# HGRN2 scores of all seven levels in one group of column-tiled products, from kept copies of keys and queries

## The chip, the cores and the metric

One Trainium2 chip, one of its cores, one launch. The metric is the device time of an execution in microseconds (us), as the median of several runs. Beside it stands one profiled execution, whose trace gives the start and the length of every instruction on every engine: PE (TensorE matmul), PEld (TensorE weight load), DVE (VectorE), ACT (ScalarE), POOL (GpSimd) and SP, the queue that issues nearly all DMAs.

## What is computed

One layer of a decoder trunk for 272 prompt positions (16 learned meta tokens and 256 prompt tokens) and 8 sampled tokens, of width 2048: a feed-forward half, a mixer, a second feed-forward half, each followed by a layer norm. All matrices are float32. The mixer projects its input to ten parts of width 2048 and runs two branches on them, retention and HGRN2, whose gated sum goes through an output projection. The change lies in HGRN2, which has 16 heads of width 128. Cut to what matters, a head computes over the prompt:

```python
b = cumsum(log f)                                   # f: forget gate, one value per position and channel
A[i, j] = sum_d q[i, d] * k[j, d] * exp(b[i, d] - b[j, d])      for j <= i, else 0
o = A @ v + (q * exp(b)) @ S                        # S: the state from earlier positions
```

The scores A are what the change touches. The decay between positions i and j differs by channel, so A isn't one product of q and k.

## The kernel before, in words

**The dense work.** Every weight matrix is streamed once, in units of eight 128x128 blocks (512 KB). SP loads a unit into `raw` (L185), ACT casts it to the reduced format `whi` (L188), DVE subtracts to get the remainder `wlo` (L189), and PE multiplies each block three times (L218: whi by xh, whi by xl, wlo by xh). Each of raw, whi and wlo has three buffers, so a unit can't be loaded, cast or subtracted before PE is done with the unit three earlier. Results go to PSUM and are evacuated by ACT and DVE.

**The mixer.** `project` (L629) walks through the parts of the input projection for eight pairs of heads, u = 0 to 7: for each pair the groups f, q_h, i_h, q_r, k_r, v_r, and then the gates of the pair before. A group is 16 steps k of `dense`; after each step `pump` (L617) is called. In the rest of the text a pump is such a step, six dense matmuls. The work of a pair that isn't dense is written as two Python generators, `mix_hg` (HGRN2) and `mix_ret` (retention). A `yield n` puts the rest of the generator off by n pumps. So the yields set, by hand, where in PE's order each small product stands; PE executes strictly in that order. The instructions of DVE, ACT, POOL and SP are put in order ahead of time by a scheduler: each engine's list follows the order of writing, but an instruction whose inputs are ready early, by the scheduler's own reckoning, may be placed earlier. On the chip each engine then works through its list in order.

**The scores.** They are built over seven levels s = 1, 2, 4, ... 64. At level s the positions fall into blocks of 2s; the queries of the second half of a block meet the keys of its first half. K and Q hold keys and queries scaled so far. After the products of a level, `scale_k(s)` and `scale_q(s)` (DVE, recorded at L240) multiply K and Q in place by the gates of that level, and `join(s)` forms the gates of the next. Because the scaling is in place, a level's products have to be done before it.

- `side_by_side(s)` (L799) copies what three levels need of Q into a tile Qm (Q1 for levels 1, 2; Q4 for 4, 8), side by side, so that one product gives three of them.
- `blocks(Q1, 1, q)` (L811, called at L859) issues, per head and half, column-tiled products: 32 columns of keys as weights, at column j of the array (tile_position (0, j)). Its second moving operand, q, gives the pairs within a block. DVE then spreads the results into the score tile acc with one product with the identity (L828) and three predicated copies (L834) for each head. `blocks(Q4, 4)` (L866) does the same for levels 4 and 8.
- Levels 16, 32 and 64 (L874 to L904) have each a PSUM bank of their own: products of 16, 32 or 64 key columns (L886, L881), the scaling, and ACT copies into acc (L899, L894). After levels 16 and 32, `load` (L765) issues two 512 KB DMAs for one of the two heads: vbh (a broadcast of sampled values) and smh (the state of the sampled sequences).

Each fp32 product is two records in the trace. The five places stand at these pumps after the generator's start, for every u: Q1 at 14, Q4 at 27, level 16 at 39, level 32 at 47, level 64 at 55. The transposes of K (L917) follow at 63, with the update of smh on ACT (L927) and DVE (L928). The tag smh has two buffers, shared by Q1, Q4 and the two smh; the tag vbh has two, for the two vbh.

**Retention beside it.** `mix_ret` is a second generator, started after v_r. It loads two smr tiles of 512 KB each for a first and again for a second half of the sampled states (L1010), vbr tiles of 256 KB (L1070), updates smr on ACT (L1106) and DVE (L1112) and writes them out (L1116). For u = 0 and u = 1 its start and that of mix_hg are set differently from the later ones (L670, L686), so that in these two pairs the two generators overlap more.

Of the kernel before, what the change touches and what calls it, by code (L numbers as in the profile page):

```python
# [14 lines left out]
ALU = mybir.AluOpType  # L15
# [3 lines left out]
P = 128  # L19
# [109 lines left out]
def trunk(ctx: ExitStack, tc: tile.TileContext, A, O):  # L129
# [417 lines left out]
    with tc.tile_pool(name="yp", bufs=1) as yp:  # L547
# [7 lines left out]
        with tc.tile_pool(name="mp", bufs=1) as mp:  # L555
# [190 lines left out]
            def mix_hg(u, f, k, q, v):  # L746
# [52 lines left out]
                def side_by_side(s):  # L799

                    x = tmp("Qm", (P, 3, 2 * P), tag="smh", bufs=2)
# [9 lines left out]
                def blocks(x, s, own=None):  # L811

                    x = x.rearrange("p i (x j c) -> p i x j c", x=4, j=4)
                    for h in range(2):
                        pl = mx_bank("pl")
                        half = pl[:, : 2 * 80].rearrange("p (b c) -> p b c", b=2)
                        for b in range(2):
                            for mine in range(1 if own is None else 2):
                                for j in range(0, P, 32):
                                    at = b * P + j  # L820
                                    o, y = half[j : j + 32, b, :48].rearrange("p (i c) -> p i c", i=3), x[:, :, 2 * h + b, j // 32, :]
                                    if mine:
                                        o, y = half[j : j + 32, b, 48:], own[:, h, at : at + 32]
                                    nc.tensor.matmul(
                                        o, K[:, h, NMETA + at : NMETA + at + 32], y, start=True, stop=True, tile_position=(0, j))
                        a = acc[:, 2 * P * h : 2 * P * (h + 1)]
                        if own is not None:
                            nc.vector.tensor_tensor(  # L828
                                out=a.rearrange("p (b j c) -> p b j c", b=2, j=4),
                                in0=half[:, :, 48:].unsqueeze(2).to_broadcast([P, 2, 4, 32]),  # L830
                                in1=ident.rearrange("p (j c) -> p j c", j=4).unsqueeze(1).to_broadcast([P, 2, 4, 32]), op=ALU.mult)
                        for i, (sl, mi) in enumerate(((s, MASKS[s][0]), (2 * s, MASKS[2 * s][0]), (2 * s, MASKS[2 * s][1]))):
                            n = 16 // sl
                            nc.vector.copy_predicated(  # L834
# [39 lines left out]
                for s in LEVELS[MASKED:]:  # L874
# [27 lines left out]
                    if s in (16, 32):  # L902
                        load(s // 32)
# [387 lines left out]
```

## Time and profile before

| | |
|---|---|
| median of 3 runs | 2581.47 us (2581.25 to 2583.45) |
| the profiled execution's own time | 2582.39 us |
| its span, first to last instruction | 2580.6 us |
| PE, PEld busy | 99%, 98% of the span |
| DVE, ACT, POOL busy | 66%, 53%, 2% |
| DMA | 536.25 MB, 208 GB/s over the span |

The span starts with the first instruction of the program; all times of the trace count from there. Matmuls are pipelined: a dense matmul's record is 0.28 us long but the next one starts about 0.12 us later, so the records overlap and the busy share of PE says little. What a piece of work costs PE is read from the distance between starts. The mixer with the input projection lies between about 780 and 1770 us.

### The profile page before, as it was taken

Reading aid. Unit: us, or ns where it says so; the run is one execution under the profiler, and the core shown is the slowest. Engines: PE = TensorE matmul, PEld = TensorE weight load, DVE = VectorE, ACT = ScalarE, POOL = GpSimd, SP = SyncE. Lnnn points to the kernel's source line nnn. Section 1 sums busy time; section 2 is a strip of 40 time slices with the busy share of each in tenths; the row PEclk is TensorE's granted clock in tenths of the full one; section 3 lists DMA queues with packets and bytes.
Section 4 is the critical chain, followed back from the end, with each engine's and each line's share of the span. In section 5 each row is a group of like instructions: output and inputs, shape, how many; then the busy total and the mean of one; then the engine's idle time right before and its main releaser. Section 6 shows DMA issues by size and latency. Waiting matters only on the chain.

```text
span 2580.6 us, 55997 instructions
## 1 busy us (share of the span) xinstructions
PE 2565.8 (99%) x23360; PEld 2540.0 (98%) x23360; DVE 1702.4 (66%) x2827; ACT 1378.0 (53%) x2146; POOL 46.4 (2%) x112
## 2 busy tenths in 40 slices
PE   9999999999999999999999999999999999999999
PEld 9999999999999999999999999999999999999998
DVE  6454454475579887777777878787985555556555
ACT  5444444444456665757575757575564444444444
POOL 0000000000000000000000000000000000000000
PEclk9999999999999999999999999999999999999999
DMA  7555555555566786767676767676666666666664
GB/s 242 182 186 184 184 187 181 188 181 184 184 200 216 248 276 208 262 211 257 213 255 216 253 220 254 215 236 195 196 186 199 196 197 195 195 194 194 196 196 149
DMA packets 156895, 536.25 MB, mean 208 GB/s; under 512 B 17952, under 2 KB 25952, under 8 KB 156640
## 3 DMA queue, kind: packets, MB, share of 16 engines
q1 hardware_dynamic: 156352, 532.37, 64.0%
q8 instruction: 183, 3.00, 0.5%
q14 instruction: 72, 0.59, 0.1%
q10 hardware_dynamic: 288, 0.29, 0.0%
HBM read 501.99 MB, written 30.61 MB: 206 GB/s over the span
## 4 chain that ended last, share of the span: by engine, by line
PE 93%; DVE 3%; DMA 2%; ACT 1%; issue 1%; SPq 0%; DVEq 0%; ACTq 0%
PE up L218 34%; PE dn L218 19%; PE pj_v_r L218 4%; PE pj_i_h L218 3%; PE pj_g_r L218 3%; PE wo L218 3%; PE pj_q_r L218 3%; PE pj_f L218 3%; PE pj_k_r L218 3%; PE pj_a_r L218 3%; PE pj_g_h L218 3%; PE pj_a_h L218 3%; PE pj_q_h L218 3%; DVE wlo L189 1%; DMA raw<-in_w_up 1%
## 5 line engine op out<-in xcount | busy, mean ns | idle before, releaser
L189 DVE TENSOR_TENSOR wlo<-raw,whi 128x1024 fp32r<-128x1024 f32 (+1 forms) x869 | 1061.8, 1222 | 762.5 <-ACT whi L188 760.8
L188 ACT CAST whi<-raw 128x1024 fp32r<-128x1024 f32 (+1 forms) x870 | 906.0, 1042 | 935.3 <-PE up L218 408.3
L218 PE MATMUL up<-xh,wlo 128*128 128x280 f32 (+1 forms) x2624 | 725.9, 280 | 1.0 <-DVE wlo L189 1.0
L218 PE MATMUL up<-xh,whi 128*128 128x280 f32 (+1 forms) x2624 | 725.7, 280 | 0.5 <-ACT whi L188 0.4
L218 PE MATMUL up<-xl,whi 128*128 128x280 f32 (+1 forms) x2624 | 725.4, 279 | 0.0
L218 PEld LDWEIGHTS up<-xh,wlo 128*128 128x128 f32 x2624 | 492.6, 189 | 1.9 <-DVE wlo L189 1.9
L218 PEld LDWEIGHTS up<-xh,whi 128*128 128x128 f32 x2624 | 492.6, 189 | 0.9 <-ACT whi L188 0.9
L218 PEld LDWEIGHTS up<-xl,whi 128*128 128x128 f32 x2624 | 492.6, 189 | 0.0
L218 PE MATMUL dn<-hh,whi 128*128 128x280 f32 (+1 forms) x1376 | 384.7, 280 | 0.0
L218 PE MATMUL dn<-hh,wlo 128*128 128x280 f32 (+1 forms) x1376 | 384.3, 279 | 0.0
L218 PE MATMUL dn<-hl,whi 128*128 128x280 f32 (+1 forms) x1376 | 384.3, 279 | 0.0
L218 PEld LDWEIGHTS dn<-hh,whi 128*128 128x128 f32 x1376 | 260.1, 189 | 0.1
L218 PEld LDWEIGHTS dn<-hl,whi 128*128 128x128 f32 x1376 | 260.1, 189 | 0.1
L218 PEld LDWEIGHTS dn<-hh,wlo 128*128 128x128 f32 x1376 | 260.1, 189 | 0.0
L218 PE MATMUL pj_g_r<-xh,whi 128*128 128x264 f32 x256 | 76.5, 299 | 0.0
L218 PE MATMUL pj_g_h<-xh,whi 128*128 128x264 f32 x256 | 74.2, 290 | 0.0
L218 PE MATMUL pj_k_r<-xh,whi 128*128 128x280 f32 x256 | 73.8, 288 | 0.0
L218 PE MATMUL pj_v_r<-xh,whi 128*128 128x280 f32 x256 | 73.4, 287 | 0.0
L218 PE MATMUL pj_v_r<-xh,wlo 128*128 128x280 f32 x256 | 72.4, 283 | 0.3 <-DVE wlo L189 0.3
L218 PE MATMUL pj_k_r<-xh,wlo 128*128 128x280 f32 x256 | 72.4, 283 | 0.0
L218 PE MATMUL pj_k_r<-xl,whi 128*128 128x280 f32 x256 | 72.3, 283 | 0.0
L218 PE MATMUL pj_v_r<-xl,whi 128*128 128x280 f32 x256 | 72.3, 283 | 0.0
(408 smaller groups left out, 5242.4 us busy)
## 6 DMA issues: line engine op xcount, KB each, us to landing
raw<-in_w_up SPq DMA_DIRECT2D x343, 512.0 KB
raw<-in_w_in SPq DMA_DIRECT2D x320, 512.0 KB
raw<-in_w_dn SPq DMA_DIRECT2D x172, 512.0 KB
smr<-in_sr SPq DMA_DIRECT2D x32, 512.0 KB
out_srs<-smr SPq DMA_DIRECT2D x32, 512.0 KB
raw<-in_w_out SPq DMA_DIRECT2D x32, 512.0 KB
smh<-in_sg SPq DMA_DIRECT2D x16, 512.0 KB
vbr<-vrd SPq DMA_DIRECT2D x32, 256.0 KB
```

The costliest lines, as they stand in the source:

```text
L188: nc.scalar.copy(hi[:, j:jn, :], raw[:, j:jn, :])
L189: nc.vector.tensor_tensor(out=lo[:, j0:j1, :], in0=raw[:, j0:j1, :], in1=hi[:, j0:j1, :].bitcast(F32), op=ALU.subtract)
L218: nc.tensor.matmul(o, w, t, start=start, stop=stop)
```

## The change

The products of all seven levels are moved to one place, pump 40 (45 for u = 0, where those of Q1 stay at pump 14). So that the scaling can go on before that, the operands of each level are kept:

- for u > 0, the products with Q1 and q take the unscaled keys k in place of K;
- a tile `kept`, in one of the two vbh buffers, holds a copy of K for levels 4 and 8 (K4) and the keys of levels 16 and 32; the queries of levels 16 and 32 go to a fourth part of Q1 and Q4 (the tile fills its buffer as smh does). These are five ACT copies for each u: one of 512 columns and four of 256;
- level 64 uses K and Q as they then are.

`upper` issues levels 16, 32 and 64, with at most 32 key columns in a product: the 64 columns of level 64 are split in two. All results share two PSUM banks. `fill` (the DVE part of the old blocks) and `keep` (the ACT copies of levels 16 to 64) come after, spread over 8 pumps; both `load` calls come right behind the products; the yields again add up to 63 pumps before the transposes of K.

```diff
-                    x = tmp("Qm", (P, 3, 2 * P), tag="smh", bufs=2)
+                    x = tmp("Qm", (P, 4, 2 * P), tag="smh", bufs=2)
...
-                def blocks(x, s, own=None):
-
-                    x = x.rearrange("p i (x j c) -> p i x j c", x=4, j=4)
+                def blocks(half, x, keys, h, own=None):
+
+                    x = x[:, :3].rearrange("p i (x j c) -> p i x j c", x=4, j=4)
...
+                                if mine:
+                                    o, y = half[j : j + 32, b, 48:], own[:, h, at : at + 32]
+                                nc.tensor.matmul(o, keys[:, h, at : at + 32], y, start=True, stop=True, tile_position=(0, j))
+
+                def fill(half, s, h):
+                    a = acc[:, 2 * P * h : 2 * P * (h + 1)]
+                    if s == 1:
+                        nc.vector.tensor_tensor(
...
+                    for i, (sl, mi) in enumerate(((s, MASKS[s][0]), (2 * s, MASKS[2 * s][0]), (2 * s, MASKS[2 * s][1]))):
...
+                def upper(pl, s, keys, qs):
+
                     for h in range(2):
                         for b in range(2):
+                            o = (h if s == 64 else 2 * h + b) * s
+                            for j in range(0, P, 2 * s):
+                                y = qs(h, b, j)
+                                for i in range(0, s, 32):
+                                    r = 64 * b + i if s == 64 else j
+                                    w = min(s, 32)
                                     nc.tensor.matmul(
-                                        o, K[:, h, NMETA + at : NMETA + at + 32], y, start=True, stop=True, tile_position=(0, j))
-                        a = acc[:, 2 * P * h : 2 * P * (h + 1)]
...
+                                        pl[r : r + w, o : o + s], keys(h, b, j)[:, i : i + w], y,
+                                        start=True, stop=True, tile_position=(0, r))
+
+                def keep(pl, s):
+                    if s == 64:
+                        for b in range(2):
+                            nc.scalar.copy(
...
-                blocks(Q1, 1, q)
+                kept = tmp("kept", (P, 4, 2 * P), tag="vbh", bufs=2)
+                K4 = kept[:, :2, :]
+                pls = [None, None]
+                first = lambda h: pls[h][:, : 2 * 80].rearrange("p (b c) -> p b c", b=2)
+                second = lambda h: pls[h][:, 2 * 80 : 2 * 128].rearrange("p (b c) -> p b c", b=2)
+                if u == 0:
+                    for h in range(2):
+                        pls[h] = mx_bank("pl")
+                        blocks(first(h), Q1, K[:, :, NMETA:], h, q)
+                        fill(first(h), 1, h)
                 scale_q(2)
                 join(2)
                 Q4 = side_by_side(4)
                 scale_k(1)
                 scale_k(2)
-                yield 2 * W_LEVEL - 1 + calm
-                blocks(Q4, 4)
+                yield W_LEVEL + calm
+                nc.scalar.copy(K4, K[:, :, NMETA:])
                 join(4)
...
-                yield W_LEVEL + 4 + calm
-                for s in LEVELS[MASKED:]:
-                    pl = mx_bank("pl")
-                    for h in range(2):
-                        for b in range(2):
-                            k0, q0, o = NMETA + b * P, b * P, (2 * h + b) * s
-                            if s == 64:
-                                j = 64 * b
...
-                                    pl[j : j + s, h * s : (h + 1) * s], K[:, h, k0 : k0 + s], Q[:, h, q0 + s : q0 + 2 * s],
...
-                                    nc.tensor.matmul(
-                                        pl[j : j + s, o : o + s], K[:, h, k0 + j : k0 + j + s],
-                                        Q[:, h, q0 + j + s : q0 + j + 2 * s], start=True, stop=True, tile_position=(0, j))
+                yield W_LEVEL
+                held = {}
+                for i, s in enumerate((16, 32)):
+                    held[s] = kept[:, 2 + i, :], (Q1, Q4)[i][:, 3, :]
+                    nc.scalar.copy(
+                        held[s][0].rearrange("p (h n s) -> p h n s", h=2, s=s),
+                        K[:, :, NMETA:].rearrange("p h (n t s) -> p h n t s", t=2, s=s)[:, :, :, 0, :])
+                    nc.scalar.copy(held[s][1].rearrange("p (h n s) -> p h n s", h=2, s=s), odd(s))
                     scale_k(s)
                     scale_q(s)
                     join(s)
-                    if s == 64:
-                        for b in range(2):
-                            nc.scalar.copy(
...
-                            nc.scalar.copy(
-                                acc[j * s : (j + 1) * s, :].rearrange("p (x n s) -> p x n s", x=4, s=s)[:, :, j + 1, :],
-                                pl[j * s : (j + 1) * s, : 4 * s].rearrange("p (x s) -> p x s", x=4))
-                    if s in (16, 32):
-                        load(s // 32)
-                    yield W_LEVEL + calm
+                    yield W_LEVEL if i == 0 or u else W_LEVEL + 5
+                for h in range(2):
+                    if u or pls[0] is None:
+                        pls[h] = mx_bank("pl")
+                        blocks(first(h), Q1, k[:, :, NMETA:], h, q)
+                if u == 0:
+                    pls = [mx_bank("pl") for h in range(2)]
+                for h in range(2):
+                    blocks(second(h), Q4, K4, h)
+                tops = {16: pls[0][:, 256:320], 32: pls[0][:, 320:448], 64: pls[1][:, 256:384]}
+                for s in (16, 32):
+                    at = lambda h, b, j: slice(128 * h + (b * P + j) // 2, 128 * h + (b * P + j) // 2 + s)
+                    upper(tops[s], s, lambda h, b, j: held[s][0][:, at(h, b, j)], lambda h, b, j: held[s][1][:, at(h, b, j)])
+                upper(
+                    tops[64], 64, lambda h, b, j: K[:, h, NMETA + b * P : NMETA + b * P + 64],
+                    lambda h, b, j: Q[:, h, b * P + 64 : (b + 1) * P])
+                scale_k(64)
+                scale_q(64)
+                join(64)
+                for h in range(2):
+                    load(h)
+                for h in range(2):
+                    if u:
+                        fill(first(h), 1, h)
+                    fill(second(h), 4, h)
+                    yield 4
+                for s in (16, 32, 64):
+                    keep(tops[s], s)
+                yield 15 if u else 10
```

47 lines of the change are left out of this document (20 added, 27 removed).

## The prediction

> **What bounds the kernel now.** I read the page first, its span and its chain of work:
>
> ```profile
> span 2580.6 us, 55997 instructions
> PE 93%; DVE 3%; DMA 2%; ACT 1%; issue 1%; SPq 0%; DVEq 0%; ACTq 0%
> ```
>
> The chain that ended last is PE for 93%. Then I read the busy time by stage, for a pair of heads in the middle of the mixer (u = 3), and PE's own waits:
>
> ```profile
> 1095.00:1223.00 128.00, 128.00 (x1271) 125.53 (x1270) 98.42 (x194) 82.14 (x152) 5.55 (x9) 1.00 0.72 236
> ...
> PE pl L881 <- DVE Q L240: 3.3, 1, 3.3
> ```
>
> The columns of the first row are length, then busy time of PE, PEld, DVE, ACT and POOL, the granted clock, DMA share and GB/s. PE has no hole in 128 us. Its longest wait of the whole span, in the second row, is one of 3.3 us in the pair u = 1. So what is taken out of PE's list for u = 2 to 7 comes off the end, as long as nothing else becomes late; for u = 0 and 1 that has to be seen.
>
> What the five places cost PE is read from the timeline of PE, u = 3: the last dense matmul before, the products, the dense matmuls after.
>
> ```profile
> 1140.96 0.28 PE L218 MATMUL pj_k_r<-xh,wlo 128*128 128x280 f32 x1
> 1141.17 0.29 PE L824 MATMUL pl<-Qm,K 128*32 128x48 f32 x8
> ...
> 1141.72 0.27 PE L824 MATMUL pl<-q,K 128*32 128x32 f32 x8
> 1141.92 0.39 PE L218 MATMUL pj_k_r<-xh,whi 128*128 128x280 f32 x1
> 1142.14 0.28 PE L218 MATMUL pj_k_r<-xl,whi 128*128 128x280 f32 x1
> ...
> 1151.08 0.28 PE L218 MATMUL pj_k_r<-xl,whi 128*128 128x280 f32 x1
> 1151.20 0.28 PE L218 MATMUL pj_k_r<-xh,wlo 128*128 128x280 f32 x1
> 1151.41 0.55 PE L824 MATMUL pl<-Qm,K 128*32 128x48 f32 x32
> 1151.89 0.39 PE L218 MATMUL pj_k_r<-xh,whi 128*128 128x280 f32 x1
> 1152.11 0.28 PE L218 MATMUL pj_k_r<-xl,whi 128*128 128x280 f32 x1
> ...
> 1160.45 0.28 PE L218 MATMUL pj_v_r<-xh,wlo 128*128 128x280 f32 x1
> 1160.67 0.39 PE L886 MATMUL pl<-Q,K 128*16 128x16 f32 x32
> 1161.20 0.28 PE L218 MATMUL pj_v_r<-xl,whi 128*128 128x280 f32 x1
> ...
> 1166.61 0.28 PE L218 MATMUL pj_a_r<-xh,wlo 128*128 128x264 f32 x1
> 1166.82 0.45 PE L886 MATMUL pl<-Q,K 128*32 128x32 f32 x16
> 1167.41 0.28 PE L218 MATMUL pj_g_r<-xl,whi 128*128 128x264 f32 x1
> ...
> 1174.93 0.28 PE L218 MATMUL pj_a_r<-xh,wlo 128*128 128x264 f32 x1
> 1175.14 0.45 PE L881 MATMUL pl<-Q,K 128*64 128x64 f32 x8
> 1175.73 0.28 PE L218 MATMUL pj_g_r<-xl,whi 128*128 128x264 f32 x1
> ```
>
> Dense matmuls start 0.12 us apart (1151.08, 1151.20), some 0.11 among the gates, which have 264 columns and not 280. From the last dense start before a group to the second one after it lie two such steps and the group's cost. Q1: 1142.14 - 1140.96 - 0.24 = 0.94. Q4: 0.91 - 0.24 = 0.67. Level 16: 0.75 - 0.24 = 0.51. Level 32: 0.80 - 0.22 = 0.58. Level 64 the same, 0.58. Together 3.28 us for each pair of heads.
>
> **The change, part by part.** *Joining the groups.* For Q4, the first product starts 0.21 after the dense one ahead of it, not 0.12, and the dense matmul behind has 0.22 to the next, not 0.12: 0.19 for going in and out. The length of one record gives the tail:
>
> ```profile
> L824 PE MATMUL pl<-Qm,K x512: 206/206/230, 817.7 to 1662.8; 128*32 128x48 f32 x171
> L834 DVE COPY_PREDICATED acch<-msk,pl x96: 283/364/508, 819.1 to 1664.2; 128x128 f32<-128x128 uint8 x96
> ```
>
> The last of the 32 records started at 1151.41 + 0.55 - 0.21 = 1151.75, so the next dense one came 0.14 behind it, while four records side by side take 0.34 / 8 = 0.04. Some 0.10 of that tail goes when another level follows at once. So a join saves 0.29, and for u = 1 to 7 there are four: 1.16. Level 64 changes from 8 records to 16. By Q4's pace (0.34 / 32) 16 records take 0.18, by their own of today (0.23 for 8) 0.46, against 0.23; I take no difference, nearest to Q4, since these too are 32-column tiles. I take **1.15 us saved per pair, between 0.9 and 1.2**; for u = 0, three joins, 0.9.
>
> *The copies.* Each pair adds five ACT copies; the nearest rows, by tile, and the stage in which they can lie, u = 5 ahead of the group:
>
> ```profile
> L755 ACT COPY K<-k x8: 627/646/659, 781.3 to 1622.9; 128x544 f32<-128x544 f32 x8
> L803 ACT COPY Qm<-Q x16: 399/418/455, 804.7 to 1635.5; 128x256 f32<-128x256 f32 x16
> ...
> 1518.00:1545.00 27.00, 27.00 (x342) 26.45 (x341) 20.60 (x43) 10.37 (x14) 2.39 (x2) 1.00 0.77 253
> 1545.00:1550.00 5.00, 5.00 (x45) 5.00 (x43) 1.79 (x3) 2.78 (x6) 0.00 (x0) 1.00 0.45 131
> 1550.00:1555.00 5.00, 5.00 (x59) 4.83 (x57) 3.77 (x6) 3.91 (x11) 0.99 (x1) 1.00 0.56 197
> ```
>
> One copy of 0.65 and four of 0.42 are 2.3 us of ACT, which is busy for 10.4 of 27 there: cost nothing, hidden by dense matmuls. Without that cover a pair pays up to 2.3. The scaling no longer waits for products when u > 0, so the chain can run early; behind a waiting ACT copy stand the whi casts.
>
> *The DVE work that moves.* The fills (12 predicated copies of 0.36 and two products with the identity of about the same for each pair, some 5.1 us by records) go from pumps 14 and 27 to pumps 40 to 48. The rows 1545 to 1555 show DVE busy for 5.56 of 10 us: 4.4 free. Four scalings of levels 16 and 32 leave that stretch, at some 0.4 each. So 5.1 comes, 1.6 goes, 4.4 is free, less the 1.15 PE gains: it fits by nothing. What is late next is the row pair
>
> ```profile
> 1574.85 1.22 DVE L189 TENSOR_TENSOR wlo<-raw,whi 128x1024 fp32r<-128x1024 f32 x1
> 1576.18 0.33 PE L218 MATMUL pj_g_r<-xh,wlo 128*128 128x264 f32 x1
> ```
>
> of the timeline: wlo ends at 1576.07, and PE uses it 0.11 later. The scalings of level 64 (0.8) also move ahead of this busy stretch, which helps. I take no stall; the bound is all that PE saves, 1.15 per pair.
>
> *The loads.* `kept` holds one vbh buffer and the fourth parts of Q1 and Q4 hold smh till the group is done, so three of the four 512 KB loads can't start sooner. Now, by SP's timeline (u = 5):
>
> ```profile
> 1518.19 1.09 SPq L769 DMA_DIRECT2D vbh<-vh0d  x1
> ...
> 1525.33 0.33 SPq L770 DMA_DIRECT2D smh<-in_sg  x1
> ```
>
> They start some 20 us sooner than they will. For u = 2 to 7 the rows above show DMA busy 0.45 and 0.56 of the time behind the group, and the loads have 23 pumps (16 us): nothing. In SP's list raw loads stand behind those waiting loads; three buffers cover them. For u = 0 and 1 it is tighter:
>
> ```profile
> 835.67 6.27 DMA smr<-in_sr
> 845.31 1.24 DVE wlo L189
> ...
> 940.94 4.14 DMA vbr<-vrd
> 948.40 0.45 PE pl L881 x8
> ...
> 831.00:847.00 16.00, 14.78 (x180) 13.91 (x179) 12.24 (x28) 12.75 (x22) 1.81 (x4) 1.00 0.92 305
> 935.00:940.00 5.00, 5.00 (x58) 4.83 (x57) 4.91 (x11) 4.94 (x9) 0.82 (x2) 1.00 0.97 355
> ```
>
> Here the chain leaves PE: for u = 0 through smr, which holds up ACT and with it whi and wlo (PE is busy 14.78 of 16, 1.2 idle); for u = 1 through vbr, which held up DVE and thereby the scaling that level 64 waited for (the 3.3). Moved out from before these waits, the loads free the smr of u = 0; moved to about 933 and 847 (estimates, where levels 16 and 32 of these two pairs stand now), 1.5 MB at 355 GB/s are 4.4 us of a DMA that is 0.92 to 0.97 busy. Level 64's own wait goes with u = 1; the same late DMA may hold up wlo instead. I count 0.6 of the 2.05 that PE saves in these two pairs, with bounds of -6.6 (all saved and both waits gone) and +4.
>
> **Sum:** 6 x 1.15 + 0.6 = 7.5. The profiled execution took 2582.4 itself, 1.8 more than its span, and so becomes 2574.9; it stood 0.9 above the median, so the median becomes **2574.0**.
>
> **The rivals.**
>
> *The waits of u = 0 and 1 go too.* For it: level 64 no longer stands behind vbr, and smr lands earlier. Against: both waits come from DMAs, which don't get fewer. 6.9 + 6.6 = 13.5, limited by what wlo allows to about 12: 2569.
>
> *The gain is eaten by DVE or by the moved loads.* The 0.11 speaks for it, and 4.4 us of DMA in each of two crowded pairs; against it the free DVE time before and the slack of later pairs. If DVE takes half in each pair and the loads the rest: about 2579; if all, 2581.5.
>
> *One long group runs at a slower pace than short ones (slower).* In place, the point is (3.28 - 0.3) / 160 = 18.6 ns per record, 160 being the records of the joined group. Q1, the longest run so far, does 64 records in 1141.72 + 0.27 - 0.2 - 1141.17 = 0.62, or 10 ns each, and speaks against it. Level 32, at 16 in 0.37 to the next dense one, shows 23 ns. If issue fell to that after the first 64, or all along, a group would take 4.0 and each pair 0.7 more: 2587.
>
> The Trainium skill, "TensorE: Matmul & The Clock Gate", section "Wait — 56ns, not 53.3ns?", says that matmuls never start closer than about 25 ns, however small. By that figure, as an estimate, 160 records take 4.0 and the time would be about 2589. This case's trace disagrees: Q1's 64 start 10 ns apart, in four column tiles.
>
> **How the numbers follow.** A measurement here can tell about 0.2% from no change, 5.2 us: faster is below 2576.3, slower above 2586.6. Forecast (2571 to 2577): 0.45, nearly all faster. Waits gone (2567 to 2571): 0.17. Eaten (2577 to 2583): 0.29. Slow pace: 0.07; other mishaps, slower: 0.02. So faster 0.62, same 0.29, slower 0.09. From 2568 to 2582 some 0.8 are held.
>
> **What would show it.** In the profile after, a group of 160 records that takes PE 2.0 to 2.3 us, once per pair; the distance of equal places of u = 3 and u = 4 down by 1.1 to 1.2; PE still without holes from 1095 on; ACT copies hidden. It is wrong if the group has gaps or a wait in its middle, if the list of PE's waits shows wlo or whi in each pair, or if waits on smr, vbr or smh in the first two pairs exceed the 4.5 us of now.

## The result, and the profile after

The changed kernel takes 2603.58 us (median of 5 runs, 2601.14 to 2606.48), the kernel before beside it 2582.12 (5 runs, 2581.25 to 2583.45): a ratio of 1.0083, with an interval of 1.0069 to 1.0096. The forecast was 2574.0, in a range of 2568 to 2582. The change makes the kernel 21.5 us slower where 8 us less was expected. The profiled execution took 2606.48 us.

The span and the chain of the page, after:

```profile
span 2604.7 us, 56181 instructions
PE 82%; DVE 7%; ACT 6%; DMA 3%; issue 2%; POOL 0%; SPq 0%; DVEq 0%; ACTq 0%
```

PE's share of the chain falls from 93% to 82%: operands now come late. PE's waits name them (total, times, longest):

```profile
PE pt L1063 <- ACT v L684: 12.0, 6, 2.6
PE pj_g_h L218 <- DVE wlo L189: 7.1, 8, 1.4
PE pt L1070 <- ACT acch L859: 1.9, 5, 0.4
PE pj_g_r L218 <- DVE wlo L189: 1.6, 2, 1.2
...
PE pt L874 <- POOL ends L751: 0.9, 2, 0.7
```

The longest is new and comes six times, once for each pair from u = 2 on: the first transpose of retention (L1063) waits for ACT to copy v_r out of PSUM (L684). A wait for wlo at L218 comes in each of these pairs too.

**The group itself** does what was forecast. PE's timeline, u = 5:

```profile
1428.18 0.28 PE L218 MATMUL pj_v_r<-xh,wlo 128*128 128x280 f32 x1
1428.39 0.29 PE L821 MATMUL pl<-Qm,k 128*32 128x48 f32 x8
...
1429.87 0.41 PE L847 MATMUL pl<-Q,K 128*32 128x64 f32 x14
1430.21 0.39 PE L218 MATMUL pj_v_r<-xh,whi 128*128 128x280 f32 x1
1430.43 0.28 PE L218 MATMUL pj_v_r<-xl,whi 128*128 128x280 f32 x1
```

From the last dense start before it to the second after it are 2.25 us; less two steps of 0.12, the group costs 2.01, against 3.28 for the five places. So 1.27 us a pair is saved. Its 160 records start within 1428.39 and 1429.87 + 0.41 - 0.24 = 1430.04: 1.65 us, 10 ns each. The Trainium skill, "TensorE: Matmul & The Clock Gate", section "Wait — 56ns, not 53.3ns?", has a floor of about 25 ns between starts; this trace disagrees for tiles of 16 and 32 columns, over 160 records as over 64.

**Where the time went** is seen from equal places of two pairs. The products of level 16, u = 4 and u = 5, before (name, times, shortest/median/longest, first and last start):

```profile
L886 PE MATMUL pl<-Q,K x32: 176/176/189, 1288.7 to 1288.9; 128*16 128x16 f32 x32
...
L886 PE MATMUL pl<-Q,K x32: 176/176/189, 1416.4 to 1416.6; 128*16 128x16 f32 x32
```

and the start of the group after for u = 4; that for u = 5 stands above, at 1428.39:

```profile
L821 PE MATMUL pl<-Qm,k x32: 206/208/231, 1296.9 to 1297.5; 128*32 128x48 f32 x32
```

A pair took 127.7 us before and takes 131.5 after. With the 1.27 saved, about 5 us of this pair are waits. (The rows of before from 1518 to 1576, which the prediction calls u = 5, are of u = 6, by the count of Q1's places in the trace; nothing in it hangs on the number.)

**What ACT does behind the group.** Its timeline before, u = 5 (start, length, and in brackets the idle time ahead and what ended it):

```profile
1420.97 0.39 ACT L684 COPY v<-pj_v_r 128x280 f32<-128x280 f32 x1 [1.63 <-PE pj_v_r L218]
1421.26 1.05 ACT L188 CAST whi<-raw 128x1024 fp32r<-128x1024 f32 x1
1422.21 0.40 ACT L685 COPY v<-pj_v_r 128x280 f32<-128x280 f32 x1
...
1434.22 0.99 ACT L927 ACTIVATE smh<-smh,fs 128x128 f32<-128x128 f32 x3
```

and after:

```profile
1431.11 1.05 ACT L188 CAST whi<-raw 128x1024 fp32r<-128x1024 f32 x1 [3.83 <-PE pj_v_r L218]
1435.40 1.28 ACT L968 ACTIVATE smh<-smh,fs 128x128 f32<-128x128 f32 x4 [3.24 <-DMA smh<-in_sg]
1436.58 1.03 ACT L188 CAST whi<-raw 128x1024 fp32r<-128x1024 f32 x1
1437.63 0.39 ACT L684 COPY v<-pj_v_r 128x280 f32<-128x280 f32 x1
1437.92 0.40 ACT L685 COPY v<-pj_v_r 128x280 f32<-128x280 f32 x1
```

Before, the updates of smh came 13 us behind the copies of v_r. Now the first four stand ahead of them, and ACT stands idle 3.24 us for the DMA that fills smh.

Two things lie behind that. The first is what lets the updates go: they are scaled by the tile `fs`, which by its tag is put into the buffer of T64, the gates of level 64. So POOL can write fs only when the scaling of level 64 has read them. That scaling now follows the group at once:

```profile
1430.76 0.42 DVE L240 TENSOR_TENSOR Q<-Q,T 128x256 f32<-128x256 f32 x1
```

POOL starts fs at 1431.24, right behind it, 6.4 us ahead of the copy of v_r; before, it started 13.0 us behind that copy. The second is the load. SP issued it only after the group, since Q1 and Q4 held its buffers (before, the two loads of smh went out at 1397.67 and 1408.38):

```profile
1429.86 0.33 SPq L770 DMA_DIRECT2D smh<-in_sg  x1
...
1430.72 0.43 SPq L770 DMA_DIRECT2D smh<-in_sg  x1
```

Issued at 1429.86, used at 1435.40: 5.5 us. Behind the waiting update stand a cast of whi, and with it a wlo, and the copies of v_r. PE's timeline shows the bill:

```profile
1435.80 0.28 PE L218 MATMUL pj_a_r<-xh,wlo 128*128 128x264 f32 x1
1438.08 0.44 PE L1063 MATMUL pt<-ident,v 128*128 128x128 f32 x2 [2.00 <-ACT v L684]
...
1442.16 0.44 PE L1070 MATMUL pt<-ident,k_r 128*128 128x128 f32 x2 [0.39 <-ACT acch L859]
...
1461.87 0.38 PE L218 MATMUL pj_g_h<-xh,wlo 128*128 128x264 f32 x1 [1.00 <-DVE wlo L189]
```

Measured by how far the same dense matmul stands behind its place in the trace of before, the steps of this pair are +2.2 at the v transposes, +0.6 at the second k transposes (a PSUM bank is free only after the score copies), +0.4 at the sums with ks, +1.2 at wlo and, ahead of the group, +0.4 at the transpose of `ends`: 4.8, less 1.27.

The same measure for every run below, from the two traces (the dense matmuls are the same in all of them). It counts from the first matmul of f of u = 0 to the output projection, cut in the group q_r of u = 2:

| run | median, us | ratio to before, with interval | u = 0 and 1, us against before | each of u = 2 to 7 |
|---|---|---|---|---|
| the changed kernel | 2603.58 | 1.0083 (1.0069 to 1.0096) | +1.0 | +3.88 |
| late_scale64 | 2587.57 | 1.0022 (1.0012 to 1.0031) | +0.3 | +0.88 |
| keep_first | 2601.58 | 1.0071 (1.0056 to 1.0086) | +1.2 | +2.94 |
| no_fill | 2602.05 | 1.0070 (1.0055 to 1.0085) | +2.5 | +2.82 |
| before_late_loads | 2582.04 | 1.0000 (0.9991 to 1.0009) | -0.2 | +0.04 |
| level64_apart | 2589.91 | 1.0035 (1.0023 to 1.0046) | +7.4 | -0.22 |
| level64_apart_no_fill | 2587.25 | 1.0021 (1.0011 to 1.0030) | +10.5 | -0.43 |
| two_groups | 2599.79 | 1.0071 (1.0054 to 1.0088) | +11.6 | +0.98 |
| before_early_updates | 2591.50 | 1.0050 (1.0028 to 1.0072) | +5.4 | +0.65 |
| gated | 2595.07 | 1.0044 (1.0031 to 1.0058) | +5.6 | +1.25 |
| gated_no_fill | 2587.66 | 1.0020 (1.0011 to 1.0029) | +7.3 | -0.32 |
| best_mix | 2581.05 | 0.9998 (0.9989 to 1.0007) | +0.6 | -0.02 |
| mix_gated12 | 2585.38 | 1.0016 (1.0007 to 1.0025) | -1.3 | +0.51 |
| mix_dve_copies | 2580.57 | 0.9989 (0.9980 to 0.9998) | +1.0 | -0.55 |
| mix_ends | 2579.51 | 0.9989 (0.9980 to 0.9998) | +0.1 | -0.41 |

The last two columns are of one profiled execution each. Ahead of the mixer, where all the kernels are the same, these executions already differ by up to 1.8 us, so 2 us in a column of sums, or 0.3 in a column of pairs, say little; some stand up to 3 us off the median of their kernel (the changed kernel 2.9 above). Of the 24 us between the two profiled executions, 23 arise in u = 2 to 7, so those pairs are what has to be explained.

### The profile page after: what moved, and what is told of

Same layout as the page of the kernel before. It is cut to its first block, busy times and chain, and to the rows that moved or that the text cites. A ratio compares the mean times of both kernels' runs of the same rounds, so it can differ in the third digit from the quotient of the medians.

```text
span 2604.7 us, 56181 instructions
## 1 busy us (share of the span) xinstructions
PE 2564.7 (98%) x23424; PEld 2536.7 (97%) x23424; DVE 1703.9 (65%) x2827; ACT 1389.3 (53%) x2186; POOL 33.9 (1%) x112
## 4 chain that ended last, share of the span: by engine, by line
PE 82%; DVE 7%; ACT 6%; DMA 3%; issue 2%; POOL 0%; SPq 0%; DVEq 0%; ACTq 0%
PE up L218 35%; PE dn L218 18%; DVE wlo L189 3%; PE wo L218 3%; PE pj_f L218 3%; PE pj_k_r L218 3%; PE pj_q_h L218 2%; PE pj_g_r L218 2%; ACT whi L188 2%; PE pj_v_r L218 2%; PE pj_g_h L218 2%; PE pj_a_h L218 2%; PE pj_a_r L218 2%; PE pj_q_r L218 2%; DMA smh<-in_sg 2%
## 5 line engine op out<-in xcount | busy, mean ns | idle before, releaser
L218 PE MATMUL up<-xh,wlo 128*128 128x280 f32 (+1 forms) x2624 | 725.9, 280 | 1.0 <-DVE wlo L189 1.0
L218 PE MATMUL up<-xh,whi 128*128 128x280 f32 (+1 forms) x2624 | 725.7, 280 | 0.3 <-ACT whi L188 0.2
L218 PE MATMUL up<-xl,whi 128*128 128x280 f32 (+1 forms) x2624 | 725.4, 279 | 0.0
L218 PEld LDWEIGHTS up<-xh,wlo 128*128 128x128 f32 x2624 | 492.5, 189 | 1.8 <-DVE wlo L189 1.8
L218 PEld LDWEIGHTS up<-xh,whi 128*128 128x128 f32 x2624 | 492.6, 189 | 0.7 <-ACT whi L188 0.7
L218 PEld LDWEIGHTS up<-xl,whi 128*128 128x128 f32 x2624 | 492.6, 189 | 0.0
L218 PE MATMUL dn<-hh,whi 128*128 128x280 f32 (+1 forms) x1376 | 384.7, 280 | 0.0
L218 PE MATMUL dn<-hh,wlo 128*128 128x280 f32 (+1 forms) x1376 | 384.3, 279 | 0.0
L218 PE MATMUL dn<-hl,whi 128*128 128x280 f32 (+1 forms) x1376 | 384.3, 279 | 0.0
L218 PEld LDWEIGHTS dn<-hh,whi 128*128 128x128 f32 x1376 | 260.1, 189 | 0.1
L218 PEld LDWEIGHTS dn<-hl,whi 128*128 128x128 f32 x1376 | 260.1, 189 | 0.1
L218 PEld LDWEIGHTS dn<-hh,wlo 128*128 128x128 f32 x1376 | 260.1, 189 | 0.0
L218 PE MATMUL pj_g_h<-xh,wlo 128*128 128x264 f32 x256 | 71.6, 280 | 7.1 <-DVE wlo L189 7.1
L218 PE MATMUL pj_g_r<-xh,whi 128*128 128x264 f32 x256 | 75.6, 295 | 0.0
L218 PE MATMUL pj_g_h<-xh,whi 128*128 128x264 f32 x256 | 73.9, 289 | 0.0
L218 PE MATMUL pj_v_r<-xh,whi 128*128 128x280 f32 x256 | 73.4, 287 | 0.0
L218 PE MATMUL pj_k_r<-xh,wlo 128*128 128x280 f32 x256 | 72.6, 283 | 0.7 <-DVE wlo L189 0.7
L218 PE MATMUL pj_g_r<-xh,wlo 128*128 128x264 f32 x256 | 71.2, 278 | 1.6 <-DVE wlo L189 1.6
L218 PE MATMUL pj_v_r<-xh,wlo 128*128 128x280 f32 x256 | 72.4, 283 | 0.3 <-DVE wlo L189 0.3
L218 PE MATMUL pj_k_r<-xh,whi 128*128 128x280 f32 x256 | 72.5, 283 | 0.0
```

What stands on the lines that cost most here:

```text
L218: nc.tensor.matmul(o, w, t, start=start, stop=stop)
```

## The experiments

**Theory A:** the scaling of level 64, now right behind the group, lets the updates of smh go some 15 pumps sooner; the scheduler puts them ahead of the copies of v_r, while the loads that they need start later. **Rivals:** B, the fills were put where DVE has no room; C, the group's PSUM banks are held until the score copies; D, late loads cost by themselves.

### The scaling of level 64 later, nothing else (late_scale64)

```diff
-                scale_k(64)
-                scale_q(64)
-                join(64)
                 for h in range(2):
                     load(h)
...
-                yield 15 if u else 10
+                yield 7 if u else 2
+                scale_k(64)
+                scale_q(64)
+                join(64)
+                yield 8
```

> The changed kernel with the scaling of level 64 and the joining of its gates 15 pumps after the products instead of right behind them. PE's list, the loads, the fills and all work stay the same; in ACT's list the updates of smh then stand behind the copies of v_r and behind the score copies, not ahead of them. Theory A (the updates of smh were let go 15 pumps earlier while their loads start later, so that ACT waits for smh ahead of the copies of v_r and of whi): the wait of the v transposes, 12.0 us in all, falls below 3 and the time to 2580 to 2592. Rival B (the fills, put on the stretch where wlo had 0.11 us of slack, cost the time): 2598 to 2604. Rival C (the PSUM banks of the group are held until the score copies): the 1.9 us at the k transposes go and little else, 2600.

Measured: 2587.57. Sixteen of the 21.5 us are gone, and with them every wait at the v transposes; the list of PE's waits now begins

```profile
PE pj_g_h L218 <- DVE wlo L189: 4.8, 8, 0.7
PE pj_g_r L218 <- DVE wlo L189: 4.7, 6, 1.2
```

and ACT's timeline shows the new order (u = 5), with PE's list, the loads and the fills written as they were:

```profile
1423.20 0.39 ACT L684 COPY v<-pj_v_r 128x280 f32<-128x280 f32 x1 [1.63 <-PE pj_v_r L218]
1423.49 1.05 ACT L188 CAST whi<-raw 128x1024 fp32r<-128x1024 f32 x1
1424.44 0.39 ACT L685 COPY v<-pj_v_r 128x280 f32<-128x280 f32 x1
1424.72 1.38 ACT L859 COPY acch<-pl 16x64 f32<-16x64 f32 x6
...
1426.95 0.40 ACT L969 ACTIVATE smh<-smh,fs 128x128 f32<-128x128 f32 x1
```

Theory A holds for the greater part. Moving three DVE instructions that nobody on PE waits for is worth 16 us, because they decide where sixteen others come to stand in a list. But the scheduler didn't leave the scaling at pump 55: DVE scales K at 1424.02 and Q at 1425.71, 4 to 6 us behind the group. So the first update still stands only 3.8 us behind the copies of v_r, not 13 as before; it waits for nothing, and wlo is late twice in each pair.

### The score copies first, and no fills (keep_first, no_fill)

keep_first puts the three `keep` calls right behind the products with the identity, ahead of the predicated copies. no_fill leaves the predicated copies out for u = 1 to 7, so that the scores of these pairs lack levels 1 to 8; it serves for the time alone:

```diff
-                    for i, (sl, mi) in enumerate(((s, MASKS[s][0]), ...
+                    for i, (sl, mi) in enumerate(() if u else ((s, MASKS[s][0]), ...
```

> The changed kernel with the ACT copies of levels 16 to 64 right behind the group, ahead of the predicated copies, so that their part of the PSUM banks is read at once. Rival C (banks held until the score copies): the k transposes wait no more (1.9 us in all) and the time falls to 2595 or less. Theory A: the updates of smh still stand ahead of the copies of v_r, so the v transposes still wait for about 12 us in all, and the time stays at 2598 to 2604. Rival B: no difference either, 2600 to 2604.

> The changed kernel with the twelve predicated copies left out for u = 1 to 7 (levels 1 to 8 are missing from the scores of these pairs), so that DVE has some 4.4 us less to do in each of seven pairs, on the stretch behind the group. Rival B (the fills cost the time): 2586 or less. Theory A: the loads and the place of the updates in ACT's list stay, so the v transposes still wait, and the time is 2594 to 2602; what it falls by is the part of the wlo waits (some 10 us in all) that DVE's load made.

Measured: 2601.58 and 2602.05, 2 and 1.5 us below the changed kernel. So neither C nor B is the main cause. In both, the wait at the v transposes falls (4.6 and 5.0 us in all, where A had it stay), but one of 5.3 us for the tails of v, which POOL copies, appears at the product behind the next k transposes: three updates instead of four stand ahead of the first copy of v_r, a cast of whi stands between the two copies, and the tails need the second.

The pair u = 7 of both runs shows something that was not planned. There PE paused 0.8 us in the middle of the group, for no reason that the trace shows, and the load was there when ACT came to it: three updates ahead of the copies of v_r, and no wait for a DMA. PE's later steps in that pair are still +2.8 (keep_first) and +2.5 us (no_fill), against +3.5 and +4.0 in u = 6, where ACT waited 1.1 and 1.8: 0.8 of it at the tails, the rest at wlo. That points to a cost of the early place by itself, to which the late load adds; it rests on one pair of one execution of each.

### Later loads in the kernel before (before_late_loads)

```diff
-                    if s in (16, 32):
-                        load(s // 32)
+                    if s == 64:
+                        load(0)
+                        load(1)
```

> The kernel before with both loads of smh and vbh issued behind the products of level 64 (pump 55) and not behind levels 16 and 32; the order of ACT's list stays that of before, with the updates behind the copies of v_r. Rival D (later loads cost by themselves, wherever the updates stand): 2598 or more. Theory A: ACT waits some 4 us for smh in each pair, but behind the copies of v_r and with up to three buffers of whi ahead, so most is covered: 2583 to 2594. If later loads cost nothing: 2581 to 2583.

Measured: 2582.04, no change. But the run does not test what it was meant to. SP's issues of smh, u = 6:

```profile
L770 SPq DMA_DIRECT2D smh<-in_sg x2: 333/380/426, 1524.2 to 1535.0; - x2
```

Before, the first was issued at 1525.33. The scheduler took the loads forward to where their buffers came free, wherever they were written. Only a buffer that is in use makes a load late here. The run says nothing on D; level64_apart does.

### Level 64 undone, with and without fills (level64_apart, level64_apart_no_fill)

```diff
-                upper(tops[64], 64, ...)
-                scale_k(64)
-                scale_q(64)
-                join(64)
...
-                for s in (16, 32, 64):
+                for s in (16, 32):
                     keep(tops[s], s)
-                yield 15 if u else 10
+                yield 7 if u else 2
+                upper(tops[64], 64, ...)
+                scale_k(64)
+                scale_q(64)
+                join(64)
+                keep(tops[64], 64)
+                yield 8
```

> The changed kernel with level 64 undone: its products, scaling and copies stand at pump 55 again, the other four places stay joined at pump 40, and so do the fills and both loads. PE saves about 0.9 us a pair against before, not 1.27. In ACT's list the updates of smh stand behind the copies of v_r, as before. Theory A with the fills as the second cost (the delayed scaling alone left waits for wlo of about 1.7 us a pair): no wait at the v transposes, wlo waits of some 1.5 us a pair remain, 2584 to 2590. If the place of the updates was all there is, 2575 to 2579. If their place was not it, 2597 or more.

> The same kernel with the twelve predicated copies left out for u = 1 to 7 (levels 1 to 8 are missing from the scores of these pairs); ACT's list has the updates behind level 64 in both. If the fills behind the group are what makes wlo late once the updates are in place, the wlo waits of the pairs go and the time is 2573 to 2578. If something else does (the scaling, the ACT copies, the loads), it stays within 2 us of the kernel with fills.

Measured: 2589.91 and 2587.25. The first is in the range that A gave, but by luck: the waits for wlo that were to make it are 0.2 a pair and not 1.5. The second fits neither range. The medians mislead, and the table's last columns tell why: the pairs u = 2 to 7 lose nothing, with or without fills (-0.22 and -0.43 a pair), and all of the loss arises in u = 0 and 1. There retention's last products wait for a DVE result (4.0 us in one place, in the trace with fills). The chain that the trace gives before that wait holds a load of smr (6.1 us), casts, wlo and eight updates of smh on DVE (2.2 us); which of them costs the time was not tested. For u = 2 to 7 rival D falls: late loads alone cost nothing. SP's and ACT's timelines, u = 5:

```profile
1422.29 0.33 SPq L770 DMA_DIRECT2D smh<-in_sg  x1
```

```profile
1439.05 0.99 ACT L970 ACTIVATE smh<-smh,fs 128x128 f32<-128x128 f32 x3
```

The load is as late as in the changed kernel, right behind the group; the update comes 17 us later, 13 us behind the copies of v_r, and waits for nothing. The fills cost little here: 0.2 a pair by the traces, which is within their scatter, and 2.7 us in all by the medians.

### Two groups, and early updates in the kernel before (two_groups, before_early_updates)

two_groups joins Q1 and Q4 at pump 27, with the fills there, and levels 16 to 64 at pump 47, from copies in one vbh buffer. before_early_updates writes the update loop, its factors and both loads behind level 16.

> The kernel before with two groups in place of five: Q1 (with the unscaled k, for u > 0) and Q4 together at pump 27 with their fills there, levels 16, 32 and 64 together at pump 47 from copies kept in one vbh buffer; the scaling of level 64 stays at pump 55, the first smh load is issued at pump 39 and the second at 47. Three joins a pair save PE some 0.9 us in u = 1 to 7 and 0.6 in u = 0, 6.9 in all. Theory A with the fills as the second cost: updates behind the copies of v_r, fills where DVE has time, smh early, so nearly all of it comes off: 2574 to 2578. If joining as such brings late operands: 2582 or more.

> The kernel before with the updates of smh written behind level 16, so that all sixteen stand ahead of the copies of v_r in ACT's list, and with both loads issued there too, which the trace of before shows landing in time (issued at 1518 and 1525 us, ahead of level 16 at 1544). Theory A (early updates cost because their loads are late): here the data are there, no wait at the v transposes over 1 us, 2580 to 2587. Rival A' (sixteen updates ahead of the copies of v_r cost as such, 5 us of ACT and DVE on that stretch): 2592 or more.

Measured: 2599.79 and 2591.50. The first lies where joining as such was to bring late operands, the second between the two ranges. two_groups loses 11.6 us in u = 0 and 1 and 0.98 in each later pair, where wlo is late at the same two places as in late_scale64. There too the first update stands close behind the copies of v_r (4.7 us) and waits for nothing. Over the runs, the pairs u = 2 to 7 follow that place: with the first update 2.2 us ahead of the copies they lose 3.88, at 1.0 ahead 2.8 to 2.9, at 3.8 and 4.7 behind 0.9 to 1.0, at 13 behind (before, level64_apart, best_mix) nothing. These runs differ in more than the place, so this speaks for A without proving that it is all. before_early_updates, with all updates 19 us ahead of the copies, loses 5.4 in the first two pairs and only 0.65 in each later one, so the distance alone is not the measure. It did not separate the early place from the late data, since the updates waited there too. ACT's timeline, u = 5:

```profile
1407.98 2.45 ACT L910 ACTIVATE smh<-smh,fs 128x128 f32<-128x128 f32 x8 [2.58 <-DMA smh<-in_sg]
...
1421.37 2.45 ACT L910 ACTIVATE smh<-smh,fs 128x128 f32<-128x128 f32 x8 [3.85 <-DMA smh<-in_sg]
```

It shows something else. These two waits, 6.4 us of ACT in the pair u = 5, stand ahead of casts of whi, of which three are buffered, and the pair is only 0.4 longer (2.4 in u = 6, the most). In the changed kernel one wait of 3.24, ahead of the copies of v_r that PE needs a few pumps later, costs 2.2 at that place alone.

### Updates held back by their data, with and without fills (gated, gated_no_fill)

```diff
-                nc.gpsimd.tensor_copy(meta[:, :, :NMETA], K[:, :, :NMETA])
+                nc.scalar.copy(meta[:, :, :NMETA], K[:, :, :NMETA])
...
-                nc.gpsimd.tensor_copy(fs, fk[:, 0])
...
+                keys(0)
+                one = tmp("one", (P, 1))
+                nc.gpsimd.tensor_scalar(
+                    out=one, in0=kts[0][:, 0, 0:1], scalar1=1.0, scalar2=1.0, op0=ALU.min, op1=ALU.max)
+                nc.vector.tensor_scalar(out=fs, in0=fk[:, 0], scalar1=one, scalar2=None, op0=ALU.mult)
...
```

`keys(0)` holds the first head's transposes, at pump 55, and fs now needs a value from them. All seven levels stay in one group; the small copy of meta moves from POOL to ACT. gated_no_fill leaves out the predicated copies as no_fill does.

> The changed kernel with its one group of seven levels, its loads and its fills as they are, but the updates of smh held back by their data: their factors fs are formed only from a value read out of the first head's transposed keys, and those transposes stand at pump 55, not 63. The scheduler can no longer put the updates ahead of the copies of v_r. The small copy of meta goes from POOL to ACT, so that it no longer stands ahead of the copies of ends. Theory A in full (what the change costs is the early place of the updates, and the waits for wlo left in the kernel with the delayed scaling come from updates still placed early): no wait at the v transposes, wlo waits of the pairs near those of before, a pair of u = 2 to 7 takes 0.8 to 1.3 us less than before, and the time is 2574 to 2579. Rival (fills behind the group, or late loads, cost by themselves): wlo waits of 1.5 us or more a pair stay and the time is 2583 or more.

> The kernel with the updates of smh held back to pump 55 by their data, with the twelve predicated copies left out for u = 1 to 7 (levels 1 to 8 are missing from the scores of these pairs). ACT's list has the updates at the same place as with the fills. With the fills that kernel lost 1.0 to 1.2 us a pair in u = 2 to 7 although PE saved 1.27: waits for wlo (0.8 a pair), for ks (0.4 to 0.7) and for the ends. If DVE's fills behind the group make those late (the rival theory for what is left), they go, and a pair gains 1 us or more against before from u = 2 on: 2580 to 2585 with the loss in u = 1 kept. If the place of the updates makes them late (now too late, bunched with those of smr), the waits stay and the time is 2590 to 2596.

Measured: 2595.07 and 2587.66. The v transposes don't wait, but gated still loses 1.25 a pair where A expected 0.8 to 1.3 saved. gated_no_fill lies between its two ranges: the waits for wlo go, as the rival had it, but a pair gains 0.3 and not 1. PE's waits with the fills:

```profile
...
PE pj_g_h L218 <- DVE wlo L189: 4.1, 12, 0.8
PE pt L874 <- POOL ends L751: 2.3, 4, 0.7
PE psr L1132 <- DVE ks L1095: 2.1, 6, 0.4
```

and without:

```profile
...
PE pt L874 <- POOL ends L751: 1.9, 4, 0.7
...
PE pj_g_h L218 <- DVE wlo L189: 1.2, 2, 0.8
```

Here the fills decide: without them a pair is 0.32 shorter than before, with them 1.25 longer, 1.57 between the two; the medians differ by 7.4. So rival B is the second cause, but only for some places of the updates: with level 64 apart the fills cost hardly anything, here, with the first update 21 us behind the copies of v_r, 1.57 a pair.

### The better pairs put together (best_mix, mix_gated12)

best_mix takes late_scale64 for u = 0 and 1 and level64_apart from u = 2 on; mix_gated12 takes the same first pairs and the held-back updates, with the first transposes at pump 51, from u = 2 on.

> For u = 2 to 7 the kernel with level 64 apart at pump 55 (its pairs 2 to 7 took as long as before or up to 0.6 us less), for u = 0 and 1 the kernel with all levels in the group and only the scaling of level 64 delayed (by the end of its pair 1 it stood 0.8 us ahead of before, where level 64 apart stood 5.6 behind). If pairs can be combined in this way: 2577 to 2581. If the loss in the first two pairs depends on what follows: 2584 or more.

> The same first two pairs; for u = 2 to 7 all seven levels in the group and the updates held back by their data, with the first head's key transposes at pump 51, so that the updates come near to where they stood before (in ACT's list one copy of whi after the transposed keys, the first smr among them). If only the place of the updates decides, the whole 1.27 us a pair comes off, less the 0.3 at the ends: 2574 to 2579. If the fills or the late loads cost by themselves, wlo waits of 1 us or more a pair remain: 2582 or more.

Measured: 2581.05 and 2585.38. best_mix is level with before: the pairs can be combined, the first two cost +0.6, but PE's 0.9 a pair still does not come off (-0.02). mix_gated12 loses at a new place, the products psc, which wait for ACT's copy of the transposed v (5.4 us in six pairs): the early key transposes brought two casts of km, 0.5 us, right ahead of it in ACT's list. The waits for wlo that the rival named did not come.

### What still eats 0.9 us a pair (mix_dve_copies, mix_ends)

In best_mix the transpose of `ends` (L874) waits in three of the pairs. POOL forms ends from the v of the i_h group (L751), and ACT copies that v out of PSUM. ACT's timeline there, u = 4:

```profile
1255.97 0.40 ACT L913 COPY Qm<-Q 128x256 f32<-128x256 f32 x1
1257.68 0.40 ACT L913 COPY Qm<-Q 128x256 f32<-128x256 f32 x1 [1.32 <-DVE Q L240]
1258.00 0.38 ACT L667 COPY v<-pj_i_h 128x280 f32<-128x280 f32 x1
```

The added copy takes 0.40 but waits 1.32 for a scaling, ahead of the copy of v. Two ways out of it: the four copies of levels 16 and 32 on DVE, or the waiting transpose one pump later.

```diff
-                    nc.scalar.copy(
+                    (nc.vector.tensor_copy if u > 1 else nc.scalar.copy)(
...
```

```diff
                     if h:
+                        if u > 1:
+                            yield 1
                         nc.tensor.transpose(x, ends ...
...
-                yield 10 + calm
+                yield 10 + calm if u < 2 else 9 + calm
```

> The kernel of best_mix with the four copies of keys and queries of levels 16 and 32 made by DVE and not by ACT, for u = 2 to 7. In best_mix a pair of u = 2 to 7 saves PE about 0.9 us and gives it back, 0.3 to 1.2 of it at the transposes behind the copy of ends (L874), which waits for the ACT copies of v of the i_h group. If the added ACT copies, which stand right ahead of those of v in ACT's list, make them late (step b of the prediction, counted at nothing), the wait at L874 goes and the time falls by 2 to 4 us: 2577 to 2579.5. If v is late for another reason: unchanged at 2580.5 to 2582, or more if DVE has no room.

> The kernel of best_mix with the one transpose that reads ends one pump later on PE, for u = 2 to 7, and nothing else changed in ACT's list but what follows from that. If a wait of 0.3 to 1.2 us a pair at this place is what keeps best_mix from being faster, it is covered by the six dense matmuls in between and the time falls by 2 to 4 us: 2577 to 2579.5. If the lateness only shows up elsewhere (at wlo): 2580.5 or more.

Measured: 2580.57 and 2579.51, beside 2582.76 of before: ratios of 0.9989 both (0.9980 to 0.9998). The wait at L874 is gone from both lists. mix_dve_copies lies where no change was forecast, but before stood higher beside it; the falls, 2.2 and 3.2 us, are of the size forecast. With the copies on DVE, ACT copies v sooner:

```profile
1257.10 0.39 ACT L667 COPY v<-pj_i_h 128x280 f32<-128x280 f32 x1 [1.30 <-PE pj_i_h L218]
```

A pair gains 0.55 and 0.41. Both are faster than both kernels, mix_ends with the lower median: by 3.2 us, a tenth of a per cent, against before, with an interval that only just leaves out no change, and by about 24 against the changed kernel. That is some 0.4 to 0.5 us a pair of the 0.9 that PE is spared; most of the rest is a wait for wlo, a step of about 0.35 at the place that the prediction named, where the slack had been 0.11. PE's timeline of mix_ends, u = 5:

```profile
1446.18 0.38 PE L218 MATMUL pj_g_r<-xh,wlo 128*128 128x264 f32 x1 [0.20 <-DVE wlo L189]
```

## Why the prediction was wrong

- **Joining the groups: right.** Forecast 1.15 us a pair (0.9 to 1.2), measured 1.27, just above that range; the group of 160 records was to take 2.0 to 2.3 and takes 2.01.
- **The scalings of level 64 "also move ahead of this busy stretch, which helps": this is the step that failed, with the wrong sign.** The move frees the buffer of fs, and with it the updates of smh, which the scheduler then puts ahead of the copies of v_r. The front of the document says that it may place earlier what it reckons ready; the prediction didn't ask what became ready. Undoing this move alone gives back 16 of the 21.5 us.
- **The loads, "23 pumps (16 us): nothing": wrong as a consequence.** The 23 pumps run to where the updates are written, pump 63. A load has as long as ACT's list gives it: ACT came to the update at about 1432.2, 2.3 us after the issue, and waited till 1435.40. The prediction looked for the work behind a *load* in SP's list and not for what stands behind a *user* of the load in ACT's list. Where the updates stay behind, the sentence is right: level64_apart loads as late and loses nothing in u = 2 to 7. In the sum, 6 x 1.15 saved became 6 x 3.88 lost.
- **The fills, "I take no stall", bound 1.15: a second cost, sized by the order.** Between next to nothing (level 64 apart) and 1.57 us a pair (gated). In the changed kernel, leaving them out makes the whole 1.5 us shorter by the medians; the traces show 1.06 a pair in u = 2 to 7, but the one of the changed kernel stands 2.9 above its median.
- **The copies, "cost nothing": nearly.** Their busy time is hidden, but one of them waits 1.32 us for DVE ahead of the copies of v; that costs 0.4 to 0.5 a pair in best_mix, by what the two ways out of it gain. The prediction named the casts of whi as what stands behind such a wait; these are buffered threefold, and it was the copies of v, which are not.
- **u = 0 and 1:** 0.6 less was counted, 1.0 more came; the bounds held it.
- **The rivals.** "Eaten by DVE or the moved loads" named both causes but ended at 2581.5, because it let them eat the gain and no more: a wait taken as bounded by PE's saving was not bounded by it. The slow pace of a long group, the one rival that ended slower, did not occur (10 ns a record against the 18.6 at which the saving would be gone).
- **What would show it:** the groups of u = 4 and u = 5 came apart by 3.8 more, those of u = 3 and u = 4 by 2.7 (starts at 1166.2 and 1296.9 after, 1160.7 and 1288.7 before), not 1.1 less, and wlo waits did appear in each pair, which the prediction had named as the sign of being wrong.

What stays open: how the loss divides between the early place of the updates and their late data. The pairs u = 7 of keep_first and no_fill speak for a cost of the early place without any wait for a load, and late_scale64 and two_groups point the same way; no run gives the changed kernel's own order with its loads in time. That would need buffers of their own for Q1, Q4 and kept, 12 KB more in each partition, and wasn't tried. Why u = 0 and 1 lose 5 to 12 us in six of the variants was not settled either.

## What to carry to other kernels

When an edit finishes something sooner, ask what that releases: where a scheduler orders the lists, the freed work may be placed ahead of instructions on the critical path, and if its data come late, all behind it in that list waits too. Time that a load has is counted up to its first user's place in the engine's list, not to the line where the user is written. An added instruction costs its own wait as well as its length. What it costs PE depended here on how well the next thing behind it is buffered.

## What the runs showed of the hardware

A load of 512 KB was there for its reader 5.5 us after its issue, with two more issued within 0.9 us behind it; in before_early_updates, u = 5, the two loads of smh took 5.9 and 6.3. Column-tiled products of all seven levels, with 16 and 32 columns of keys and 16 to 64 moving columns, follow one another in one group of the changed kernel without a gap that the records show: 160 in 1.65 us. In four of the variants the group of u = 7 had a pause of 0.5 to 0.8 us in it, of which the trace names no cause. The rest was order, not hardware.
